# Expert parts that follow each other by halves of gate and up, and one-hot tables on VectorE

## The chip, the cores and the metric

The kernel runs on one core of a Trainium2 chip. The metric is the device time of one execution in microseconds. The kernel before takes 1694.38 us, the median of 3 runs (1686.91 to 1696.34).

The core has five engines that run beside each other, each through its own queue of instructions in order: TensorE (PE, matrix products, with its weight loads as PEld), VectorE (DVE), ScalarE (ACT), GpSimd (POOL) and SyncE (SP, which here only issues transfers). They meet through semaphores.

## The reference

One decoder block over 512 tokens of width 1024: a mixer (state-space scan and short convolution), then a mixture of experts with 64 experts, 8 for each token, expert width 256, and one shared expert. The change touches the experts alone. What they compute, shortened:

```python
scores = sigmoid(hf @ router_w)                       # 512 x 64
_, e_idx = lax.top_k(masked(scores + router_bias), 8)  # groups: 4 of 8 allowed
gate = take(scores, e_idx); gate = gate / gate.sum() * 2.5
def expert_block(xb, e):                               # rows of one expert
    return (silu(xb @ w_gate[e]) * (xb @ w_up[e])) @ w_down[e]
routed = segment_sum(yb * row_gate, row_tok)           # back to the tokens
shared = (silu(hf @ sh_gate) * (hf @ sh_up)) @ sh_down
x = layer_norm(ALPHA * x + g2 * (routed + shared)) * ln2_g + ln2_b
```

In float32, an expert's gate and up weights are 2 x 1 MB and its down weight 1 MB: 192 MB for the 64 experts, each read once.

## The kernel before

**Stages.** The mixer, the router and the shared expert fill the first 855 us or so. The routed experts run from about 876 to 1663 us, and the last layer norm ends the span.

**Parts and units.** The experts are ranked by their number of tokens, and each rank has a fixed number of rows (`CAPS`, L35). One tile of PE has 128 rows, so experts of few rows share a tile. A part is named by a letter: `q` is four experts of 32 rows in one tile, `p` two of 64, `a` one of 96 with one of 32, `f` one of 128; `y` is one expert of 192 rows, and `z` one of 160, each as a full tile of 128 (its block of one expert) and a second tile that it shares with another expert; `x` is the largest with three tiles. A unit is a few parts that are worked together: L41 names them, as `qy`, `ap` or `qff`. A static unit of experts 0 and 1 goes first. A block is one tile of rows, and a unit has one to four.

**What a unit does on PE**, in an order written by hand (`unit`, L1399, under the manual schedule of L1426): the products with gate and up (the first stage of `ffn`, L953 to L972), then, interleaved, the combination of the unit before (`csteps`, L1170, its products L1180 and L1181), this unit's transposes (`act_t`), and the gathering and transposing of the next unit's rows (`slots` L1101, `xs_steps` L1345), and then the products with the down weights. The gate and up products sum over K = 1024 in eight steps of 128, by quarters of two steps: a loop over four quarters `q` (L960), and in each all blocks of the unit, in the order of the unit in even quarters and backwards in odd ones. Blocks of several experts use plain products (`tiled`, L950, written to `ps_pj` or, for a fourth block, to `ps_y`). Blocks of one expert split each weight into a high and a low part (`split`, ACT L158 then DVE L160, three sets of buffers) and use three fast products for each step (L153, L154, L155). The other engines' instructions are ordered by a scheduler.

**Weights.** An expert's weights come in three pieces of 1 MB: half 0 and half 1 of gate and up (two transfers of 512 KB, L869) and down (L872). SP issues them in the order of the plan (`plan`, `take`; L1337 to L1339): all half-0 pieces of a unit, then all half-1 pieces, then all downs. There are buffers for nine pieces (seven `pr` and two more that every eighth piece takes), so a piece waits on SP until the one eight places before it has been read. Up to `AHEAD` = 10 are asked for early. The number of a routed expert is loaded on SP into a register (L1273) before its pieces can be issued.

**Rows in and out.** For each block DVE makes a one-hot table of the slots (`oh`, L1108), PE reduces it (L1116), DVE forms `idx` (L1121), and GpSimd issues the indirect transfer that gathers the rows (L1124). When a block's down product is done, `done` (L1143) makes on GpSimd a token number (`tok`, L1152) and the one-hot table `oht` of 128 x 512 (L1153) with which the next unit's combination adds the rows to the tokens. `oht` has three buffers, and one comes free when the combination that reads it has ended.

The line on which the order of a part's blocks rests, and the two on GpSimd:

```python
for o, (xh, xl), b in list(zip(os_, xs, blocks))[::-1 if q % 2 else 1]:
    ...
GP.tensor_scalar(tok, red[:, 0:1], NOTOK, None, op0=OP.add)
GP.tensor_scalar(res_[b][0], iota_t, tok, None, op0=OP.is_equal)
```

## Time and profile before

| | |
|---|---|
| median of 3 runs | 1694.38 us (1686.91 to 1696.34) |
| profiled execution | 1693.0 us |
| its span | 1691.2 us, mean granted clock of PE 0.95 |
| busy: PE, DVE, ACT, POOL | 1527.4, 962.3, 642.4, 315.9 us |

The profile is of one execution. Its span is 1.8 us shorter than that execution's own time, and the median of the three runs is 1.4 us longer than the profiled execution. Each row of a timeline below gives start and length in us, the engine and the line of the kernel, output and input by the program's names, and in square brackets the idle time just before the instruction with what ended it. PE's granted clock stands as a share of its full 2.4 GHz.

### The profile page before, as it was taken

How to read it: one execution, taken by the hardware profiler on the slowest of the kernel's cores; microseconds unless marked ns; L12 is line 12 of the kernel's file. 1: busy time of each engine (PE TensorE's matmuls, PEld its weight loads, DVE VectorE, ACT ScalarE, POOL GpSimd, SP SyncE). 2: the span in 40 equal slices, each digit the busy share in tenths (PEclk: the TensorE clock that was granted, in tenths of full speed). 3: DMA queues.
4: the chain of work that ended last, by engine and by line, in shares of the span. 5: the costliest groups of instructions: out<-in, count | busy, mean ns of one | idle time of the engine just before them, and what ended most of it. 6: DMA issues, size and time to landing. Idle time of an engine off the chain costs nothing.

```text
span 1691.2 us, 22909 instructions
## 1 busy us (share of the span) xinstructions
PE 1527.4 (90%) x8253; PEld 1024.9 (61%) x8253; DVE 962.3 (57%) x1728; ACT 642.4 (38%) x925; POOL 315.9 (19%) x314
## 2 busy tenths in 40 slices
PE   6999999999999999999887779997889988999894
PEld 4687787777878777877654344444434444544452
DVE  4558767777676666267853434345354453444445
ACT  3557656655535454344422222123231222212222
POOL 0011101101004566000350120221022211022111
PEclk9999999999999999999898879998799989999997
DMA  9663434425315576253537478776688769787671
GB/s 277 154 173 78 110 90 97 115 76 159 69 47 163 176 247 188 87 189 142 191 101 260 144 264 333 287 287 227 258 302 297 278 240 361 282 312 279 243 307 51
DMA packets 194504, 335.67 MB, mean 198 GB/s; under 512 B 13428, under 2 KB 136660, under 8 KB 186196
## 3 DMA queue, kind: packets, MB, share of 16 engines
q1 hardware_dynamic: 183300, 303.73, 52.7%
q0 software_dynamic: 11088, 30.45, 7.0%
q8 instruction: 66, 1.08, 0.3%
q14 instruction: 50, 0.41, 0.1%
HBM read 334.58 MB, written 4.28 MB: 200 GB/s over the span
## 4 chain that ended last, share of the span: by engine, by line
PE 68%; DMA 13%; DVE 7%; issue 6%; ACT 3%; POOL 2%; SPq 1%; DVEq 0%; POOLq 0%; ACTq 0%
PE ps_pj L153 12%; PE ps_pj L154 11%; PE ps_pj L155 11%; PE ps_pj L950 8%; DMA pr<-in_w_up_dram 6%; PE ps_y L950 5%; PE ps_tr L150 4%; PE ps_y L1180 4%; PE ps_y L1181 4%; DMA pg<-h_d,idx 4%; DMA pg<-in_w_ada_dram 2%; PE ps_y L153 1%; DVE wl L160 1%; PE ps_y L483 1%; POOL pg L366 1%
## 5 line engine op out<-in xcount | busy, mean ns | idle before, releaser
L153 PE MATMUL ps_pj<-hm,wh 128*128 128x512 f32 x680 | 274.9, 405 | 1.6 <-ACT wh L158 1.6
L155 PE MATMUL ps_pj<-hm,wl 128*128 128x512 f32 x680 | 266.7, 393 | 5.3 <-DVE wl L160 5.3
L154 PE MATMUL ps_pj<-hm,wh 128*128 128x512 f32 x680 | 266.6, 392 | 0.0
L950 PE MATMUL ps_pj<-pr,xt 128*32 128x512 f32 (+1 forms) x1472 | 226.4, 609 | 26.1 <-DMA pr<-in_w_up_dram 25.4
L160 DVE TENSOR_TENSOR wl<-pg,wh 128x1024 fp32r<-128x1024 f32 (+1 forms) x129 | 159.3, 1241 | 112.7 <-ACT wh L158 112.4
L160 DVE TENSOR_TENSOR wl<-pr,wh 128x1024 fp32r<-128x1024 f32 x72 | 85.9, 1221 | 163.2 <-ACT wh L158 163.2
L158 ACT ACTIVATE wh<-pg 128x1024 fp32r<-128x1024 f32 (+1 forms) x135 | 127.5, 952 | 132.2 <-PE ps_pj L154 98.9
L950 PEld LDWEIGHTS ps_pj<-pr,xt 128*32 128x32 f32 (+1 forms) x1472 | 61.8, 117 | 173.0 <-issue 167.4
L1153 POOL TENSOR_SCALAR oht<-iota_t,tok 128x512 fp32r<-128x512 f32 x41 | 76.9, 1879 | 472.6 <-PE ps_y L1181 470.5
L153 PEld LDWEIGHTS ps_pj<-hm,wh 128*128 128x128 f32 x680 | 128.0, 188 | 35.9 <-issue 6.6
L155 PEld LDWEIGHTS ps_pj<-hm,wl 128*128 128x128 f32 x680 | 127.9, 188 | 34.7 <-DVE wl L160 7.0
L154 PEld LDWEIGHTS ps_pj<-hm,wh 128*128 128x128 f32 x680 | 128.2, 188 | 28.8 <-issue 3.4
L158 ACT ACTIVATE wh<-pr 128x1024 fp32r<-128x1024 f32 x72 | 73.3, 1051 | 180.0 <-DMA pr<-in_w_down_dram 80.8
L150 PE MATMUL ps_tr<-ident,pg 128*128 128x128 f32 x392 | 72.2, 318 | 64.1 <-DMA pg<-h_d,idx 60.2
L1186 DVE TENSOR_TENSOR res<-res,ps_y 128x512 f32<-128x512 f32 x120 | 82.2, 686 | 56.2 <-PE ps_y L1181 55.0
L950 PE MATMUL ps_y<-pr,wkr 128*32 128x512 f32 (+1 forms) x736 | 111.8, 643 | 0.8 <-DVE wk L1157 0.8
L150 PEld LDWEIGHTS ps_tr<-ident,pg 128*128 128x128 f32 x392 | 59.7, 197 | 77.3 <-issue 44.2
L1157 DVE SCALAR_TENSOR_TENSOR wk<-ps_y,red,pg 128x512 f32<-128x512 f32 x82 | 60.8, 748 | 44.4 <-PE ps_y L155 25.9
L366 POOL TENSOR_TENSOR pg<-pg 128x1024 f32<-128x1024 f32 x28 | 75.4, 2708 | 53.7 <-ACT pg L364 53.7
L1124 POOL DMA_INDIRECT pg<-h_d,idx x41 | 46.4, 1132 | 177.2 <-issue 120.6
L153 PE MATMUL ps_pj<-pg,wh 128*128 128x512 f32 x192 | 75.9, 395 | 1.1 <-ACT zs L431 1.1
L155 PE MATMUL ps_pj<-pg,wl 128*128 128x512 f32 x192 | 76.2, 397 | 0.0
(394 smaller groups left out, 2682.0 us busy)
## 6 DMA issues: line engine op xcount, KB each, us to landing
pr<-in_w_gate_dram SPq DMA_DIRECT2D x128, 512.0 KB, 7.9
pr<-in_w_up_dram SPq DMA_DIRECT2D x128, 512.0 KB, 8.7
pr<-in_w_down_dram SPq DMA_DIRECT2D x64, 1024.0 KB, 11.0
pg<-in_w_in_dram SPq DMA_DIRECT2D x88, 512.0 KB, 6.2
pg<-in_w_ada_dram SPq DMA_DIRECT2D x48, 512.0 KB, 5.7
bc<-acs_d POOLq DMA_DIRECT2D x32, 256.0 KB, 4.2
pg<-in_w_ssd_out_dram SPq DMA_DIRECT2D x16, 512.0 KB, 4.5
pg<-in_w_sc_out_dram SPq DMA_DIRECT2D x8, 512.0 KB, 4.1
```

The source lines that it names most:

```text
L150: return PE.transpose(o, i, ident[:n, :n])
L153: PE.matmul(o, lh, rh, start=start, stop=False)
L154: PE.matmul(o, lh, rl, start=False, stop=False)
L155: PE.matmul(o, ll, rh, start=False, stop=stop)
L158: S.activation(hi, src, AF.Copy)
L160: V.tensor_tensor(lo, src, rw(hi), op=OP.subtract)
L366: GP.tensor_tensor(part[i], part[i], w, op=OP.add)
L950: PE.matmul(o[w * i:w * i + w, :], x[:, w * i:w * i + w], m, start=start, stop=stop, tile_position=(0, w * i))
L1153: GP.tensor_scalar(res_[b][0], iota_t, tok, None, op0=OP.is_equal)
L1180: PE.matmul(o, oh_, yh[:, ns_], start=(i == 0), stop=False)
L1181: PE.matmul(o, oh_, yl[:, ns_], start=False, stop=(i == len(ps_) - 1))
L1186: V.tensor_tensor(ra[t][:, ns_], ra[t][:, ns_], o, op=OP.add)
```

## The change

Each part of a unit is now a list of blocks (`subs`), and `halves_of` orders the gate and up products: every part does its half 0 of K (four steps) in turn, and then every part its half 1 in reverse order of parts and blocks. The splits of both quarters of a half are asked for before its products. A block's activation (`act_in`) follows its half 1 at once, so that the activations come in that order too. The plan asks for the pieces of a unit in the order in which the halves come, and for all downs behind them. `tok` and `oht` are made on VectorE (`V`) instead of GpSimd (`GP`). The shared expert and the static unit go through the same function, with one part. In the diff below three one-line hunks are left out, which pass the new argument.

```diff
--- before.py
+++ after.py
@@ -950,34 +950,42 @@
             PE.matmul(o[w * i:w * i + w, :], x[:, w * i:w * i + w], m, start=start, stop=stop,
                       tile_position=(0, w * i))
 
-    def ffn(blocks, xs, w, done, gp=False):
+    def halves_of(subs):
+
+        return [(s_, 0) for s_ in subs] + [(s_[::-1], 1) for s_ in subs[::-1]]
+
+    def ffn(blocks, subs, xs, w, done, gp=False):
+
 
 
 
         es = sorted({e for b in blocks for e in b})
         split_e = sorted({b[0] for b in blocks if len(b) == 1})
         os_ = [bank(*(("pj", 3) if i < 3 else ("y", 2))) for i in range(len(xs))]
-        for q in range(4):
-            uq = {e: w(e, q) for e in es}
-            hl_ = {e: split(uq[e], GP if gp else None) for e in split_e}
-            for o, (xh, xl), b in list(zip(os_, xs, blocks))[::-1 if q % 2 else 1]:
-                for k in (2 * q, 2 * q + 1):
+        sgs = {}
+        for s_, h in halves_of(subs):
+            uq = {(e, q): w(e, q) for e in sorted({e for i in s_ for e in blocks[i]}) for q in (2 * h, 2 * h + 1)}
+            hl_ = {eq: split(u, GP if gp else None) for eq, u in uq.items() if eq[0] in split_e}
+            for i in s_:
+                o, (xh, xl), b = os_[i], xs[i], blocks[i]
+                for k in range(4 * h, 4 * h + 4):
                     if len(b) == 1:
-                        wh, wl = hl_[b[0]]
+                        wh, wl = hl_[b[0], k // 2]
                         matmul3(o, xh[:, k, :], xl[:, k, :], wh[:, :, k % 2, :], wl[:, :, k % 2, :], k == 0, k == KD - 1)
                     else:
-                        tiled(o, xh[:, k, :], [uq[e][:, :, k % 2, :] for e in b], k == 0, k == KD - 1)
-            if q == 3:
-                sgs = [act_in(o) for o in os_]
+                        tiled(o, xh[:, k, :], [uq[e, k // 2][:, :, k % 2, :] for e in b], k == 0, k == KD - 1)
+                if h:
+                    sgs[i] = act_in(o)
             yield
-        acts = []
-        for sg, b in zip(sgs, blocks):
-            acts.append(act_t(sg, len(b) > 1))
+        acts = {}
+        for i, sg in sgs.items():
+            acts[i] = act_t(sg, len(blocks[i]) > 1)
             yield
         yield
         us = [{e: w(e, 4 + j) for e in es} for j in range(2)]
         wdn = {e: [split(us[j][e], GP if gp else None) for j in range(2)] for e in split_e}
-        for i, ((ah, al), b) in enumerate(zip(acts, blocks)):
+        for i, b in enumerate(blocks):
+            ah, al = acts[i]
             for n in range(2):
                 o = bank("y", 2)
                 ns_ = slice(n * 512, (n + 1) * 512)
@@ -1136,7 +1144,7 @@
 
     npart, tail = [0], [False]
 
-    def expert(blocks, sl_, xs, w):
+    def expert(blocks, subs, sl_, xs, w):
 
         res_ = []
@@ -1149,8 +1157,8 @@
                 res_.append((rt.tile([P, T], FR, name="oht", bufs=3), *ring[i]))
                 npart[0] += 1
                 tok = rt.tile([P, 1], F32, name="tok", bufs=2)
-                GP.tensor_scalar(tok, red[:, 0:1], NOTOK, None, op0=OP.add)
-                GP.tensor_scalar(res_[b][0], iota_t, tok, None, op0=OP.is_equal)
+                V.tensor_scalar(tok, red[:, 0:1], NOTOK, None, op0=OP.add)
+                V.tensor_scalar(res_[b][0], iota_t, tok, None, op0=OP.is_equal)
             _, yh, yl = res_[b]
             ns_ = slice(n * 512, (n + 1) * 512)
             yg = wk()
@@ -1162,7 +1170,7 @@
             if n == 1:
                 parts.append(res_[b])
 
-        return ffn(blocks, xs, rows_of(w), done)
+        return ffn(blocks, subs, xs, rows_of(w), done)
 
     parts = []
     rsum = rt.tile([P, NT, 2], F32, name="rsum")
@@ -1323,20 +1331,22 @@
                              [(tuple(range(m)), lambda r=r, n=n, m=m: slots(seg(r, n, m)))]))
     for ks in ORDER.split():
 
-        rs, bl = (), []
+        rs, bl, subs = (), [], []
         for k in ks:
             r_, b_ = kinds[k].pop(0)
+            subs.append(list(range(len(bl), len(bl) + len(b_))))
             bl += [(tuple(len(rs) + e for e in es), sl_) for es, sl_ in b_]
             rs += r_
-        units.append((rs, bl))
+        units.append((rs, bl, subs))
     assert not any(kinds.values())
     ublk, allb = {}, []
     for n, u in enumerate(units):
         ublk[n] = len(allb)
         allb += u[1]
-        for q in range(3):
-            for i, r in enumerate(u[0]):
-                plan((n, i, q), lambda r=r, q=q: expert_piece(rank(r), q))
+        if u[0]:
+            for i, q in [(i, h) for s_, h in halves_of(u[2]) for i in sorted({e for b in s_ for e in u[1][b][0]})] \
+                    + [(i, 2) for i in range(len(u[0]))]:
+                plan((n, i, q), lambda r=u[0][i], q=q: expert_piece(rank(r), q))
     xs = []
 
     def need_s(n):
@@ -1403,8 +1413,8 @@
         i0, i1 = ublk[n], ublk[n] + len(units[n][1])
         i2 = i1 + len(units[n + 1][1]) if n + 1 < len(units) else i1
         need_x(i1)
-        run = expert([b for b, _ in units[n][1]], sl[i0:i1], xs[i0:i1], lambda e, q: take((n, e, q), AHEAD))
-        for _ in range(4):
+        run = expert([b for b, _ in units[n][1]], units[n][2], sl[i0:i1], xs[i0:i1], lambda e, q: take((n, e, q), AHEAD))
+        for _ in range(2 * len(units[n][2])):
             next(run)
         com = csteps() if parts else iter(())
         for _ in range(2):
```

The first place is PE at the start of the first `ap` unit after the static one: the downs of `ya`, then all gate and up products of `ap` (64-row products are those of `p`, 32-row products those of `a`; `ps_y` holds downs, `ps_pj` gate and up, `xt` the gathered rows). Before:

```order
L950 MATMUL ps_y<-pr,wkr 64x512 x8
L950 MATMUL ps_y<-pr,wkr 32x512 x16
L950 MATMUL ps_pj<-pr,xt 32x512 x8
L950 MATMUL ps_pj<-pr,xt 64x512 x8
L950 MATMUL ps_pj<-pr,xt 32x512 x16
L950 MATMUL ps_pj<-pr,xt 64x512 x8
L950 MATMUL ps_pj<-pr,xt 32x512 x8
L1180 MATMUL ps_y<-rww,oht 128x512
```

And after:

```order
L950 MATMUL ps_y<-pr,wkr 64x512 x8
L950 MATMUL ps_y<-pr,wkr 32x512 x16
L950 MATMUL ps_pj<-pr,xt 32x512 x16
L950 MATMUL ps_pj<-pr,xt 64x512 x16
L950 MATMUL ps_pj<-pr,xt 32x512 x16
L1188 MATMUL ps_y<-rww,oht 128x512
L1189 MATMUL ps_y<-pg,oht 128x512
```

The first 32-row stretch has doubled, the two 64-row stretches have become one, and the pieces of half 1 of `a` are needed last instead of in the third and fifth stretch.

The second place is DVE behind the combination in the unit `qy` (`res` is the running sum of a token tile, `red` and `idx` belong to the slots of the next unit, `wl` to a split). Before:

```order
L1186 TENSOR_TENSOR res_75<-res_75,ps_y 128x512
L1119 TENSOR_REDUCE red<-ps_st 128x2
L1108 TENSOR_TENSOR oh<-iota_5824,pgt 128x512
L1121 TENSOR_SCALAR idx<-red 128x1
L160 TENSOR_TENSOR wl_79<-pr,wh_78 128x1024
L1186 TENSOR_TENSOR res_75<-res_75,ps_y 128x512
L1119 TENSOR_REDUCE red<-ps_st 128x2
L160 TENSOR_TENSOR wl_81<-pr,wh_80 128x1024
L1121 TENSOR_SCALAR idx<-red 128x1
```

And after:

```order
L1194 TENSOR_TENSOR res_75<-res_75,ps_y 128x512
L1127 TENSOR_REDUCE red<-ps_st 128x2
L1116 TENSOR_TENSOR oh<-iota_5824,pgt 128x512
L1129 TENSOR_SCALAR idx<-red 128x1
L1161 TENSOR_SCALAR oht<-iota_t,tok 128x512 x2
L1194 TENSOR_TENSOR res_75<-res_75,ps_y 128x512
L160 TENSOR_TENSOR wl_79<-pr,wh_78 128x1024
L1127 TENSOR_REDUCE red<-ps_st 128x2
L1160 TENSOR_SCALAR tok<-red 128x1
L160 TENSOR_TENSOR wl_81<-pr,wh_80 128x1024
L1129 TENSOR_SCALAR idx<-red 128x1
L1161 TENSOR_SCALAR oht<-iota_t,tok 128x512
```

Two tables stand behind the first `idx` and ahead of the last sum of the combination, and a third behind the second `idx`. On POOL, where tables and gathers took turns, nothing but the gathers is left.

The third place is SP before the routed experts (`L869` and `L872` are pieces of the static unit, `eidx` the list of expert numbers). Before:

```order
L869 DMA pr<-in_w_up_dram 128x1024
L872 DMA pr<-in_w_down_dram 128x2048 x2
L1273 TENSOR_LOAD eidx
L1273 ISA x2
L869 REGISTER_ALU
L869 ISA
L869 DMA pr<-in_w_gate_dram 128x1024
```

And after:

```order
L869 DMA pr<-in_w_up_dram 128x1024
L1281 TENSOR_LOAD eidx
L1281 ISA x2
L1281 TENSOR_LOAD eidx
L1281 ISA x2
L1281 TENSOR_LOAD eidx
L1281 ISA x2
L1281 TENSOR_LOAD eidx
L1281 ISA x2
L1281 TENSOR_LOAD eidx
L1281 ISA x2
L1281 TENSOR_LOAD eidx
```

Six loads of expert numbers, which wait for `eidx`, now stand ahead of the other three gate and up pieces and the two downs of the static unit.

## Rows read from the trace of the kernel before

**Rows 1.** The page: the span and the busy times of the engines.

```profile
span 1691.2 us, 22909 instructions
...
PE 1527.4 (90%) x8253; PEld 1024.9 (61%) x8253; DVE 962.3 (57%) x1728; ACT 642.4 (38%) x925; POOL 315.9 (19%) x314
```

**Rows 2.** Busy time of each engine in three stretches: the routed experts, the gate and up products of `qy`, and those of `qff`. The columns are start and end, length, busy us and count of PE, PEld, DVE, ACT and POOL, PE's granted clock, the share of the transfer engines that is busy, and GB/s.

```profile
900.00:1660.00 760.00, 671.69 (x4048) 359.83 (x4048) 337.20 (x562) 191.81 (x307) 118.79 (x110) 0.92 0.73 270
953.60:989.60 36.00, 27.65 (x123) 9.48 (x121) 4.63 (x6) 3.27 (x4) 0.00 (x0) 0.81 0.64 234
1169.50:1212.90 43.40, 31.72 (x116) 15.20 (x108) 11.43 (x11) 8.64 (x9) 0.00 (x0) 0.69 0.64 228
```

**Rows 3.** What PE waited for between 900 and 1660 us: us in total, times, longest.

```profile
PE ps_tr L150 <- DMA pg<-h_d,idx: 52.0, 10, 8.1
PE ps_pj L950 <- DMA pr<-in_w_up_dram: 25.4, 14, 6.5
PE ps_pj L153 <- ACT wh L158: 3.8, 4, 2.3
PE ps_pj L154 <- DVE wl L160: 2.6, 5, 0.8
```

**Rows 4.** The timeline of PE in the gate and up products of `qff`, up to the first product of the combination (L1180). L950 is `q`, L153 to L155 are the two `f`.

```profile
1169.46 1.90 PE L950 MATMUL ps_pj<-pr,xt 128*32 128x512 f32 x16
1173.63 0.50 PE L153 MATMUL ps_pj<-wh,xt 128*128 128x512 f32 x1 [2.27 <-ACT wh L158]
...
1193.05 1.89 PE L950 MATMUL ps_pj<-pr,xt 128*32 128x512 f32 x2 [4.58 <-DMA pr<-in_w_up_dram]
1196.12 3.59 PE L950 MATMUL ps_pj<-pr,xt 128*32 128x512 f32 x10 [1.19 <-DMA pr<-in_w_up_dram]
...
1211.08 1.92 PE L950 MATMUL ps_pj<-pr,xt 128*32 128x512 f32 x16
1212.93 0.50 PE L1180 MATMUL ps_y<-pr,oht 128*128 128x512 f32 x1
```

**Rows 5.** The timeline of SP's queue in the same stretch: the last half-0 piece, the first transfer of the half-1 pieces of `q`, and the downs behind them.

```profile
1172.06 0.34 SPq L869 DMA_DIRECT2D pr<-in_w_up_dram  x1
1187.63 0.33 SPq L869 DMA_DIRECT2D pr<-in_w_gate_dram  x1
...
1193.48 22.36 SPq L872 DMA_DIRECT2D pr<-in_w_down_dram  x6
```

**Rows 6.** The timeline of PE in the gate and up products of `qy`: the second tile of `y` (64 columns) in one quarter, and `q`'s waits.

```profile
957.03 3.65 PE L950 MATMUL ps_pj<-pr,xt 128*64 128x512 f32 x16
...
971.44 1.89 PE L950 MATMUL ps_pj<-pr,xt 128*32 128x512 f32 x2 [6.46 <-DMA pr<-in_w_up_dram]
974.71 3.59 PE L950 MATMUL ps_pj<-pr,xt 128*32 128x512 f32 x10 [1.39 <-DMA pr<-in_w_up_dram]
```

**Rows 7.** The timeline of PE: the first and the last of the ten waits for a weight of gate and up in the other units.

```profile
1041.04 1.49 PE L950 MATMUL ps_pj<-pr,xt 128*32 128x512 f32 x12 [0.79 <-DMA pr<-in_w_up_dram]
...
1609.53 2.78 PE L950 MATMUL ps_pj<-pr,xt 128*32 128x512 f32 x24 [1.54 <-DMA pr<-in_w_up_dram]
```

**Rows 8.** What POOL waited for between 860 and 1660 us, the largest entry: us in total, times, longest.

```profile
POOL oht L1153 <- PE ps_y L1181: 470.5, 11, 62.2
```

**Rows 9.** The timeline of POOL: the issue of a gather (DMA_INDIRECT) in the unit before `qy`, and a table with the gather behind it in `qy`.

```profile
936.67 0.99 POOL L1124 DMA_INDIRECT pg<-h_d,idx  x1 [31.67 <-PE ps_st L1116]
...
1003.03 2.63 POOL L1153 TENSOR_SCALAR oht<-iota_t,tok 128x512 fp32r<-128x512 f32 x1 [57.22 <-PE ps_y L1181]
1005.82 1.14 POOL L1124 DMA_INDIRECT pg<-h_d,idx  x1 [0.16 <-issue]
```

**Rows 10.** The timeline of DVE: the indices of those two gathers.

```profile
935.78 0.15 DVE L1121 TENSOR_SCALAR idx<-red 128x1 int32<-128x1 f32 x1
...
1002.92 0.15 DVE L1121 TENSOR_SCALAR idx<-red 128x1 int32<-128x1 f32 x1
```

**Rows 11.** The timeline of PE: the transposes that wait for the second of them.

```profile
1011.32 1.94 PE L150 MATMUL ps_tr<-ident,pg 128*128 128x128 f32 x8 [6.83 <-DMA pg<-h_d,idx]
```

**Rows 12.** Groups of DVE instructions of one line and shape in the whole span: count, busy us, mean ns of one, idle us before them.

```profile
L468 DVE TENSOR_SCALAR esc<-bc,acs 128x128 f32<-128x128 f32 x128 | 29.9, 292 | 6.1 <-DMA bc<-acs_d 5.4 <-PE ps_y L483 0.7
L258 DVE TENSOR_SCALAR pg<-pg,mv,rstd 128x1024 f32<-128x1024 f32 x4 | 3.2, 804 | 0.0
L1121 DVE TENSOR_SCALAR idx<-red 128x1 int32<-128x1 f32 x41 | 6.1, 148 | 0.1
```

**Rows 13.** The timeline of SP's queue at the first routed pieces: between the second and the third transfer stands one load of an expert's number.

```profile
856.28 0.36 SPq L869 DMA_DIRECT2D pr<-in_w_gate_dram  x1
856.90 0.34 SPq L869 DMA_DIRECT2D pr<-in_w_up_dram  x1
858.17 0.34 SPq L869 DMA_DIRECT2D pr<-in_w_gate_dram  x1
```

**Rows 14.** The timeline of PE: the first gate and up product of the static unit.

```profile
876.13 1.93 PE L950 MATMUL ps_pj<-pr,xt 128*64 128x512 f32 x6
```

**Rows 15.** The page's groups: the two steps of a weight's split.

```profile
L160 DVE TENSOR_TENSOR wl<-pr,wh 128x1024 fp32r<-128x1024 f32 x72 | 85.9, 1221 | 163.2 <-ACT wh L158 163.2
...
L158 ACT ACTIVATE wh<-pr 128x1024 fp32r<-128x1024 f32 x72 | 73.3, 1051 | 180.0 <-DMA pr<-in_w_down_dram 80.8
```

**Rows 16.** A short stretch with a brief wait for a weight, in the columns of rows 2.

```profile
1085.00:1095.00 10.00, 9.14 (x39) 3.76 (x40) 1.25 (x3) 0.66 (x2) 0.00 (x0) 0.83 0.94 383
```

More of the change, by code (lines that the diff above doesn't have):

```diff
@@ L1226, in done @@
             GP.tensor_tensor(ra[ts[b]][:, ns_], ra[ts[b]][:, ns_], tm, op=OP.add)
-        drain(ffn([[0]] * len(ts), [mt[t] for t in ts], lambda e, q: shw[q], done, len(ts) > 1))
+        drain(ffn([[0]] * len(ts), [list(range(len(ts)))], [mt[t] for t in ts], lambda e, q: shw[q], done, len(ts) > 1))
     def static_slots(u):
@@ L1302, in block_kernel @@
     of = {c: [r for r in range(E - NST) if caps[r] == c] for _, c in CAPS}
-    units = [((), [(tuple(range(len(u))), lambda u=u: static_slots(u))]) for u in STAT]
+    units = [((), [(tuple(range(len(u))), lambda u=u: static_slots(u))], [[0]]) for u in STAT]
     kinds = {c: [] for c in "xyzfapq"}
@@ L1503, in block_kernel @@
         blk = slots((pv[:, :, None], P, [po]))
-        drain(expert([[0]], [blk], [xsplit(blk[0])], lambda e, q: expert_piece(bass.ds(er, 1), q)))
+        drain(expert([[0]], [[0]], [blk], [xsplit(blk[0])], lambda e, q: expert_piece(bass.ds(er, 1), q)))
         combine(True)
```

## The prediction

> **What bounds the kernel now.** I read the page first. PE is busy 1527 of 1691 us [rows 1], so some 164 us can be won at most, and a change of the experts only finds its part of it between 900 and 1660 us. There PE is busy 672 of 760 us; DVE has 337 us of work and is free for 423, POOL has 119, and the transfers take 0.73 of their engines' time [rows 2]. No engine but PE is full over the whole stretch. Then I read what PE waits for there [rows 3]: 52 us for gathered rows (ten times), 25 us for weights of gate and up (14 times), and 6.4 us for splits. The last stretches to read are the two units with four experts in `q`, because the granted clock is 0.81 in the gate and up products of `qy` and 0.69 in those of `qff`, against 0.92 over all routed experts [rows 2]. A level of 0.5 (1.2 GHz) thus holds for much of both. So a wait costs twice there: once itself, and again in slower products behind it.
>
> **Gate and up of `qff`.** They take from 1169.46 to 1212.93, that is 43.5 us [rows 4]. PE alone at full clock needs 18.7: four quarters of `q` at 1.9 (the row of 16 products), and for each `f` 24 split products of 0.232 us (the distance from start to start of the fast ones), two times 5.6. The loss begins with the weights. Six half-0 pieces come first, and the half-1 pieces of `q` need the buffers from which half 0 of `q` is read. With the quarters taken in turn, that half is read out only when the second quarter of `q` ends, and SP issues the first of them at 1187.63 [rows 5]. PE waits from 1188.5 to 1193.05, once more to 1196.12, and then goes on at half speed [rows 4]. After the change `q` does its two quarters of half 0 in one go, from 1169.5 to 1173.3, so those four buffers come free 14.3 us earlier, while both `f` are worked. The transfers do not follow by as much. The last half-0 piece is issued at 1172.06 [rows 5] and three to four pieces of 1.05 MB are still on their way. At 383 to 400 GB/s, the rate of a full stretch [rows 16], a piece takes 2.7 us; four behind four are done some 20 us after 1171, at about 1192. One half of `q`, 3.8 us, may follow the last: 1196 to 1198 in place of 1212.9. I take 15 us less. The best is PE alone with the first split in its way, 23 less. The worst has splits as the limit: eight pairs of DVE subtractions at 1.22 us [rows 15] are 19.5 us, from 1173 to 1192, and `q` at half clock behind them, 7.6, would end at 1200; with a late piece, 10 less.
>
> **Gate and up of `qy`.** They take 36.0 us [rows 2]; PE alone needs 7.6 for `q`, 5.6 for the full tile of `y` and 7.3 for its second tile, 3.65 for each of two quarters' worth of pairs [rows 6], 20.5 in sum. Half 0 of `q` would be read out at 957.4 and its pieces' successors issued from there, before the 12.9 us of `y`, which end at 970.3. The four pieces (10.5 us behind some that are on the way) would be in at about 972, and the end at 976 and not at 989.6: 13 us less. At most 15, which is PE alone; at least 6, if only the wait of 6.46 goes [rows 6].
>
> **The other waits for weights.** Ten in seven units, such as 0.79 in the first and 1.54 in the last [rows 7]. When the four of `qff` and `qy` are taken from the 25.4 us of rows 3 (4.58, 1.19, 6.46 and 1.39), 11.8 are left. In an `ap` unit the second part's weights of half 1 are wanted before those of the first, and the gap between half 0 of `a` and its half 1 grows by a whole part, 3.65 us; a weight that was late by 0.8 to 1.5 us would then be in time. A stretch with such a wait ran at 0.83 [rows 16], so a little clock returns. I take 9, with bounds of 3 and 15.
>
> **Tables off POOL.** POOL runs its queue in order. A table waits for its buffer, which the last product of the combination frees: 470 us in eleven waits [rows 8]. A gather behind it is late though its index is there. In the unit before `qy` an index begins at 935.78 and its gather is issued at 936.67, 0.9 later; in `qy` an index begins at 1002.92, two-and-a-half microseconds of table follow, and the gather goes at 1005.82, 2.9 later [rows 9, 10]. PE waits for its rows until 1011.32, for 6.83 us [rows 11]. So 2.0 of that go. I did the same for each of the ten waits in rows 3: six gathers stand behind a table, with 1.0 to 2.7 us lost, 10 in all; four lose nothing. The rest of the 52 us is the gather's own latency and stays. I take 10; none if something else holds the gather, and 13 with the clock.
>
> **Tables on DVE.** 41 tables of 128x512 from one operand. No row has this operation on DVE; its like took 292 ns at a quarter of the size and 804 ns at twice it [rows 12], so I take 0.5, and the token number as 0.15. All on the path that would be 27 us. They are covered: DVE is free for 423 of 760 us [rows 2], and behind the combination, where they stand, PE waits for the gather, not for DVE. The first index stands ahead of the first two tables, so it isn't late; the second index stands behind them, by 1.0 to 1.6 us, less than a table took on POOL. I take 0, bounds 0 and 5.
>
> **SP before the routed experts.** Six loads of an expert's number move ahead of five pieces of the static unit. One costs the distance from 856.90 to 858.17 [rows 13], less that of a plain pair (0.62), some 0.65 us; with a bound of 0.93 the five extra ones are 3.3 to 4.7 us. The pieces that now go out by 840 would go out from about 860 and, at 2.7 us each, be in by 871 to 874; the first product that wants one is at 876.13 [rows 14], and downs come later. So 0, up to 5 if the clear space of 2 to 5 us is used up.
>
> **Order of splits and activations.** A half asks for two pairs of splits with three sets of buffers, in the shared expert, too; and the activations come backwards, which the combination hides. I take 1 more, between 1 less and 4 more.
>
> The sum goes against the profiled execution's 1693.0: less 15, 13, 9 and 10, plus 1, is 46 less, 1647. The median stands 1.4 higher, hence 1648. With every best bound it is 67 less, 1627; with every worst, 5 less, 1689.
>
> **A rule from the skill.** A gather issued beside a DVE split of 1.22 us took 1.14 us against 0.99 [rows 9], and that split has two operands in the SBUF. The Trainium skill, page "SBUF — State Buffer", section "SBUF: two separate sides", says that a DVE operation in a two-port mode keeps GpSimd from writing the descriptors of its transfers; page "VectorE: DVE Perf Modes", section "The perf-mode tier table", gives such a mode to `tensor_scalar` on float32. By that rule the two tables just behind an index would hold up the gather that the index has released. No row shows this pair; what it would take is below.
>
> **Rivals.**
> Transfers stay the limit in the six-expert units. For it: the half-1 pieces come in a queue that is already full at 383 GB/s [rows 16]. Against: over these two stretches the share is 0.64 [rows 2]. Then half of 28 and 3 of 9 remain: 1668.
> More returns: no wait for weights is left, and the clock stays up. All best bounds: 1628.
> Two tables beside the gather's issue take back the 2.0 us that it won: no gain at the gathers, and so 1658. The rule above is the reason; only 0.15 us is seen so far.
> Nothing comes of it: the waits only gather elsewhere, since a combination that starts earlier meets the same gathers and downs still on their way (they go out in a run of 22 us, [rows 5]); about 1690.
> Slower: splits. A full tile now wants two quarters' splits at once, with three sets; if the scheduler starts them only when the part begins, PE stands for a whole chain of ACT and DVE, about 2.5 us (1.05 and 1.22 for each of two, overlapped [rows 15]; the wait at 1173.63 was 2.27 [rows 4]). Twelve experts with full tiles, two halves each: 60 us. It decides when the chains aren't ahead in more than three quarters of the cases: 1693 less 46 plus 60, with the 1.4, is 1708. Against it: all splits together cost PE 6.4 us so far [rows 3], and the wait of 2.27 stood behind a late weight.
>
> **How the numbers follow.** Forecast 46% (its own range 1638 to 1661), transfers 20%, tables beside the gather 8%, more returns 10%, nothing 9%, slower 7%. About 0.5% (8.5 us, 1686 to 1703) is what a measurement of this kernel can tell from no change. Faster by more has the first four, 84%; same 9%; slower 7%. The range leaves out the slower case and half of the extreme ones: 1628 to 1686.
>
> **What would show it.** In the changed profile: the SP timeline of `qff` should issue `q`'s half-1 pieces about 4 us behind the first product, not 18; the stretch from the first product to the combination should be near 28 us, with a clock above 0.8, and that of `qy` near 23. PE's waits for gate and up should be under 8 us in place of 25, those for gathers near 42. POOL should wait for no table. Splits should cost PE no more than 10 us. If gathers are issued over 1.5 us behind their index, the rule on ports is at work; if the downs or the gathers wait longer than before, the gain went there, and I am wrong.

## The result and the profile after

The changed kernel takes 1629.8 us, the median of 4 runs (1629.3 to 1630.8); the kernel before took 1692.2 in the same comparison. The ratio is 0.963, with a 95% interval of 0.960 to 0.966. The profiled execution took 1629.3 us, and its span is 63.7 us shorter. 1648 was forecast, so the direction and the range held (1628 to 1686), but the gain was 62 us and not 46.

The page of the changed kernel, as [rows 1]:

```profile
span 1627.5 us, 22863 instructions
...
PE 1496.8 (92%) x8253; PEld 1018.3 (63%) x8253; DVE 974.6 (60%) x1810; ACT 645.4 (40%) x925; POOL 230.3 (14%) x232
```

PE executes the same 8253 products and is busy 30.6 us less, so about half of the gain is products that run at a faster clock. The windows of the changed kernel over the routed experts, `qy` and `qff`, in the columns of [rows 2], show where: the clock is 0.94 and 1.00 where it was 0.81 and 0.69.

```profile
900.00:1600.00 700.00, 639.24 (x4034) 353.32 (x4033) 354.15 (x637) 195.45 (x308) 39.17 (x35) 0.96 0.78 293
945.80:973.30 27.50, 24.52 (x122) 9.29 (x120) 5.52 (x8) 4.04 (x6) 0.00 (x0) 0.94 0.94 352
1141.20:1167.60 26.40, 21.11 (x116) 11.03 (x108) 12.34 (x13) 9.67 (x11) 0.00 (x0) 1.00 1.01 380
```

PE's waits in the changed kernel between 900 and 1600 us, as [rows 3] (the routed experts end 64 us earlier now, hence the shorter stretch): weights 9.7 us instead of 25.4, gathered rows 43.7 instead of 52.0, splits 5.7 instead of 6.4.

```profile
PE ps_tr L150 <- DMA pg<-h_d,idx: 43.7, 11, 5.4
PE ps_pj L950 <- DMA pr<-in_w_up_dram: 9.7, 8, 1.6
PE ps_pj L154 <- DVE wl L160: 4.8, 6, 1.0
...
PE ps_pj L153 <- ACT wh L158: 0.9, 2, 0.5
```

Then I cut both timelines of PE at the first product of each stage (gate and up, combination, downs) and took the lengths from one to the next:

| stage | before | after | change, us |
|---|---|---|---|
| start of the static unit | 876.1 | 877.3 | +1.1 |
| static unit to `x` | 30.5 | 19.8 | -10.7 |
| `x` | 47.0 | 48.8 | +1.8 |
| gate and up of `qff` | 43.5 | 26.5 | -17.0 |
| gate and up of `qy` | 36.0 | 27.5 | -8.5 |
| gate and up of the other units | 237.9 | 222.9 | -15.0 |
| combinations behind `x`, with transposes and gathers | 252.5 | 240.1 | -12.4 |
| downs behind `x` | 137.7 | 134.4 | -3.3 |
| sum | | | -64.0 |

Each column is one execution. The start of the static unit alone lies anywhere from 875.5 to 884.4 us in the profiles of this study, so a difference of 1 or 2 us in one row says little.

The timeline of PE in the gate and up products of `qff` in the changed kernel, as [rows 4]:

```profile
1141.16 3.62 PE L950 MATMUL ps_pj<-pr,xt 128*32 128x512 f32 x32
1145.28 0.49 PE L153 MATMUL ps_pj<-wh,xt 128*128 128x512 f32 x1 [0.50 <-ACT wh L158]
...
1161.47 1.04 PE L950 MATMUL ps_pj<-pr,xt 128*32 128x512 f32 x2 [1.60 <-DMA pr<-in_w_up_dram]
1164.10 3.59 PE L950 MATMUL ps_pj<-pr,xt 128*32 128x512 f32 x26 [1.58 <-DMA pr<-in_w_up_dram]
1167.62 0.51 PE L1188 MATMUL ps_y<-pr,oht 128*128 128x512 f32 x1
```

And SP's queue there, as [rows 5]: the first and the last transfer of `q`'s four half-1 pieces, and the downs.

```profile
1144.78 0.34 SPq L869 DMA_DIRECT2D pr<-in_w_gate_dram  x1
...
1153.33 0.34 SPq L869 DMA_DIRECT2D pr<-in_w_up_dram  x1
1155.06 12.91 SPq L872 DMA_DIRECT2D pr<-in_w_down_dram  x6
```

The first half-1 piece of `q` goes out 3.6 us behind the first product, where it was 18.2. PE still waits for the last of them, two times 1.6 us, and here the clock stays up behind them: the last 26 products take 3.59 us where 10 took that long in [rows 4]. In `qy` it does not stay up behind waits of this length, as is shown further down.

### The profile page after: what moved, and what is told of

Its sections match the earlier page's. It is cut to its first block, busy times and chain, and to the rows that moved or that the text cites. A ratio compares the mean times of both kernels' runs of the same rounds, so it can differ in the third digit from the quotient of the medians.

```text
span 1627.5 us, 22863 instructions
## 1 busy us (share of the span) xinstructions
PE 1496.8 (92%) x8253; PEld 1018.3 (63%) x8253; DVE 974.6 (60%) x1810; ACT 645.4 (40%) x925; POOL 230.3 (14%) x232
## 4 chain that ended last, share of the span: by engine, by line
PE 68%; DMA 12%; DVE 8%; issue 6%; ACT 3%; POOL 1%; SPq 1%; DVEq 0%; ACTq 0%; POOLq 0%
PE ps_pj L153 12%; PE ps_pj L154 12%; PE ps_pj L155 12%; PE ps_pj L950 6%; DMA pr<-in_w_up_dram 5%; PE ps_y L950 5%; PE ps_y L1188 4%; PE ps_y L1189 4%; PE ps_tr L150 4%; DMA pg<-h_d,idx 4%; DMA pg<-in_w_ada_dram 2%; DVE wl L160 2%; PE ps_y L153 1%; PE ps_y L155 1%; PE ps_y L154 1%
## 5 line engine op out<-in xcount | busy, mean ns | idle before, releaser
L153 PE MATMUL ps_pj<-hm,wh 128*128 128x512 f32 x680 | 276.3, 407 | 2.0 <-ACT wh L158 2.0
L155 PE MATMUL ps_pj<-hm,wl 128*128 128x512 f32 x680 | 267.4, 394 | 6.2 <-DVE wl L160 6.2
L950 PE MATMUL ps_pj<-pr,xt 128*32 128x512 f32 (+1 forms) x1472 | 212.2, 604 | 9.7 <-DMA pr<-in_w_up_dram 9.7
L950 PEld LDWEIGHTS ps_pj<-pr,xt 128*32 128x32 f32 (+1 forms) x1472 | 62.0, 117 | 150.1 <-issue 139.7
L153 PEld LDWEIGHTS ps_pj<-hm,wh 128*128 128x128 f32 x680 | 128.9, 190 | 36.7 <-issue 6.0
L155 PEld LDWEIGHTS ps_pj<-hm,wl 128*128 128x128 f32 x680 | 128.5, 189 | 36.7 <-DVE wl L160 8.8
L950 PE MATMUL ps_y<-pr,wkr 128*32 128x512 f32 (+1 forms) x736 | 106.1, 618 | 0.8 <-DVE wk L1165 0.8
L927 ACT ACTIVATE sg<-ps_pj 128x256 f32<-128x256 f32 x44 | 16.8, 384 | 159.7 <-PE ps_pj L950 99.2
L153 PE MATMUL ps_pj<-pg,wh 128*128 128x512 f32 x192 | 76.0, 396 | 1.3 <-ACT zs L431 1.2
L155 PE MATMUL ps_pj<-pg,wl 128*128 128x512 f32 x192 | 76.3, 397 | 0.0
```

What stands on the lines that cost most here:

```text
L153: PE.matmul(o, lh, rh, start=start, stop=False)
L155: PE.matmul(o, ll, rh, start=False, stop=stop)
L950: PE.matmul(o[w * i:w * i + w, :], x[:, w * i:w * i + w], m, start=start, stop=stop, tile_position=(0, w * i))
```

## The experiments

**The order alone, the tables alone.** In the first, the new order has the tables back on GpSimd; in the second, the kernel before has them on VectorE.

```diff
-                V.tensor_scalar(tok, red[:, 0:1], NOTOK, None, op0=OP.add)
-                V.tensor_scalar(res_[b][0], iota_t, tok, None, op0=OP.is_equal)
+                GP.tensor_scalar(tok, red[:, 0:1], NOTOK, None, op0=OP.add)
+                GP.tensor_scalar(res_[b][0], iota_t, tok, None, op0=OP.is_equal)
```

> The new order of parts, with the one-hot tables left on GpSimd. Theory: the two halves of the change add up, and the order is worth what the stages of gate and up lost in the changed kernel: 17 us in qff, 8.5 in qy and some 15 in the other units, about 41 of the 62, so 1651 us with 1692 before; the static stage before the unit x should again last about 30 us from its first gate and up product to that of x, and PE should wait for gathers as before, about 52 us. Rival: the static stage and the gathers got faster because the weights come in another order and leave the transfer engines free at other times, and the tables matter little; then this kernel takes about 1632 us and the static stage about 20 us.

> The old order of parts, with the one-hot tables on VectorE. Theory: the gathers no longer stand behind tables; the static stage loses about 10 us and the combinations about 12, so some 22 less than before: 1670 us; qff keeps its 43.5 us of gate and up. Rival (the weights' order frees the transfer engines): about 1690 us, static stage still 30 us.

The order alone: 1649.0 us, ratio 0.975 (0.972 to 0.978), 42 us by the ratio and 43 by the medians. The tables alone: 1677.6 us, 0.993 (0.991 to 0.995), 12 us by the ratio and 15 by the medians, where 22 were expected. Together that is 54 to 58 of the 62, the rest within the intervals. The waits between 900 and 1600 us part as foretold, the order alone first:

```profile
PE ps_tr L150 <- DMA pg<-h_d,idx: 53.4, 10, 8.1
PE ps_pj L950 <- DMA pr<-in_w_up_dram: 11.0, 11, 2.0
```

and then the tables alone:

```profile
PE ps_tr L150 <- DMA pg<-h_d,idx: 45.6, 10, 6.8
PE ps_pj L950 <- DMA pr<-in_w_up_dram: 22.5, 11, 5.0
```

The order took the weights' waits, the tables the gathers'. Cut in the same way as in the table above, the order alone has 27.5 us in `qff`, 27.2 in `qy`, 223.9 in the other gate and up products and 252.9 in the combinations; the tables alone have 43.0, 33.2, 231.6 and 244.8. So the order has nearly all of its gain in gate and up. The tables have theirs in the combinations, but 6 us in the other gate and up products too.

One thing fits neither theory: the static stage was 23.7 us in both. The order alone still makes the tables on GpSimd there, but in its profile the second one took 1.65 us, where it took 2.71 before:

```profile
885.20 1.65 POOL L1161 TENSOR_SCALAR oht<-iota_t,tok 128x512 fp32r<-128x512 f32 x1
```

So its first gather left only 0.29 us behind the first weight and landed after 8.9 us; what this says comes below. Why the table was shorter is not shown.

**The other two corners.** Order of work and order of pieces are two edits. In the third kernel PE works in the new order and the pieces come in the old one; in the fourth PE works by quarters and the pieces come in the new order. The tables are on VectorE in both.

```diff
-            for i, q in [(i, h) for s_, h in halves_of(u[2]) for i in sorted({e for b in s_ for e in u[1][b][0]})] \
-                    + [(i, 2) for i in range(len(u[0]))]:
-                plan((n, i, q), lambda r=u[0][i], q=q: expert_piece(rank(r), q))
+            for q in range(3):
+                for i, r in enumerate(u[0]):
+                    plan((n, i, q), lambda r=r, q=q: expert_piece(rank(r), q))
```

> The changed kernel with the pieces planned as before (all half 0, all half 1, all downs) while PE works in the new order. Theory A (the order of the pieces is needed too): in qff the pieces of half 1 of f stand behind four of q in SP's queue, and PE wants them first, so qff loses 8 to 14 of its 17 us and qy some 5, with a few us in the others: 1645 to 1655. Theory B (only the early reading of half 0, which frees the buffers, counts): within 5 us of the changed kernel, 1628 to 1635.

```diff
-        for s_, h in halves_of(subs):
-            uq = {(e, q): w(e, q) for e in sorted({e for i in s_ for e in blocks[i]}) for q in (2 * h, 2 * h + 1)}
+        for q in range(4):
+            uq = {e: w(e, q) for e in es}
...
```

> The fourth corner: PE works by quarters as before, the pieces come in the new order, and the tables are on VectorE. Theory (order of work and order of pieces only help together): PE wants half 1 of q in the third quarter, but it is last in SP's queue and needs the buffers of half 0, so the waits for weights are longer than in the kernel with the tables alone (1678): 1690 to 1720. Rival (the order of the pieces is the whole gain): about 1640.

1698.0 us (ratio 1.004, 1.001 to 1.006) and 1714.6 us (1.012, 1.008 to 1.015). Either edit alone loses where both win 48: beside the 1677.6 of the tables alone, the loss is 20 and 37 us (18 and 32 by the ratios). Both theories about the third kernel missed the time. Theory A was right where it named a size: `qff` takes 36.0 us, 9.5 more than in the changed kernel, and `qy` 34.3, 6.8 more. But the other gate and up products, for which it had a few us, take 270.0, and that is 47 more. All of PE's waits for weights there are 44.8 us in 21 waits, where the changed kernel has 9.7 in 8. In `qff` PE stands before the second half of an `f`:

```profile
1188.99 0.79 PE L153 MATMUL ps_pj<-wh,xt 128*128 128x512 f32 x1 [11.48 <-ACT wh L158]
```

ACT waits there for the piece that is behind four of `q` in the queue; the row names ACT, but the weight is what came late. In the fourth kernel, too, most of the loss lies outside of the place that was named. `q` does wait in the third quarter of `qff`, but `qff` takes 43.6 us and took 43.0 with the tables alone. The other gate and up products take 269.5 in place of 231.6, and 7 and 8 us of that are in the two `faa` units, where half 1 of `f` is wanted in the third quarter and now comes last. PE's row names ACT, and ACT's row the weight:

```profile
1413.63 0.79 PE L153 MATMUL ps_pj<-wh,xt 128*128 128x512 f32 x1 [7.15 <-ACT wh L158]
```

```profile
1412.52 2.00 ACT L158 ACTIVATE wh<-pr 128x1024 fp32r<-128x1024 f32 x2 [14.41 <-DMA pr<-in_w_up_dram]
```

**The static stage.** The first four tables alone (static unit and `x`) are put on VectorE in the kernel before.

```diff
-                GP.tensor_scalar(tok, red[:, 0:1], NOTOK, None, op0=OP.add)
-                GP.tensor_scalar(res_[b][0], iota_t, tok, None, op0=OP.is_equal)
+                (V if npart[0] <= 4 else GP).tensor_scalar(tok, red[:, 0:1], NOTOK, None, op0=OP.add)
+                (V if npart[0] <= 4 else GP).tensor_scalar(res_[b][0], iota_t, tok, None, op0=OP.is_equal)
```

> The kernel before with the first four one-hot tables alone (those of the static unit and of x) on VectorE. Theory: the static stage (first gate and up product of the static unit to that of x) loses 30.5 us to about 20 to 24, because its first gather no longer stands behind two tables on GpSimd and goes out ahead of the weights that the static unit's products release, and all later units stay as before: 1682 to 1686 us with 1692 before. Rival: the short static stage of the changed kernel comes from the pieces that are issued later there, not from the tables; then 1692 and 30 us.

1685.3 us, ratio 0.994 (0.992 to 0.996), and the static stage is 23.7 us; what else brings it to 19.8 when the order is changed too was not tried. By the ratios that is 10 us (6 to 14) for four tables of 41, and 12 (8 to 16) for all of them, so the first four have most of the gain. The profiled execution (1695.6 us) is the longest of this kernel's eight: its static stage is 6.8 us shorter than before, but starts 5.0 later, so it shows the stage and not where the 10 us of the median lie. The first gather of `x` tells why the stage is shorter. Before, it left behind a table, at 882.83, when the static unit's products had already released weights, the first at 881.48; the row of transfers gives 12.8 us from its issue to its landing:

```profile
882.83 1.67 POOL L1124 DMA_INDIRECT pg<-h_d,idx  x1 [0.17 <-issue]
```

```profile
881.48 0.34 SPq L869 DMA_DIRECT2D pr<-in_w_gate_dram  x1
```

```profile
pg<-h_d,idx POOLq DMA_INDIRECT x1, 12.8
```

After, it left at 881.56, the first weight at 882.44, and it landed in 6.2:

```profile
881.56 1.52 POOL L1132 DMA_INDIRECT pg<-h_d,idx  x1 [4.29 <-DVE tok L1160]
```

```profile
882.44 0.33 SPq L869 DMA_DIRECT2D pr<-in_w_gate_dram  x1
```

```profile
pg<-h_d,idx POOLq DMA_INDIRECT x1, 6.2
```

To try this by itself, the changed kernel got two operations ahead of that one gather, which write the buffer that the gather overwrites and so can't fall behind it.

```diff
+        if nblk[0] == 1:
+            for i in range(2):
+                GP.tensor_scalar(xg[:, i * T:(i + 1) * T], iota_t, red[:, 0:1], None, op0=OP.add)
```

> The changed kernel with two extra operations of 128x512 on GpSimd right ahead of the first gather of the static stage (they fill the buffer that the gather then overwrites), some 3.4 us, as the two tables were there before. In the kernel before, that gather was issued 1.35 us behind the first weight that the static unit's products released, and landed after 12.8 us; in the changed kernel it was issued 0.88 us ahead of it and landed after 6.2. Theory (behind the weights it waits for them, so 3.4 us on GpSimd cost twice that): landing 11 to 13 us, static stage 26 to 30 us in place of 19.8, 6 to 10 us more in all, 1636 to 1640. Rival (the landing depends on something else of the old order): landing 6 to 8 us, static stage 22 to 23 us, 3 us more.

1637.0 us, 7 more than the changed kernel; the ratio is 0.968 (0.963 to 0.972), and its interval overlaps that of the changed kernel. The stages are clearer than the sum: the static stage is 28.8 us, 9.0 more, and `x` behind it 45.1, 3.7 less. In the order of time, from its timelines: the first weight, the gather, the transposes.

```profile
884.43 0.33 SPq L869 DMA_DIRECT2D pr<-in_w_gate_dram  x1
```

```profile
882.57 3.16 POOL L1133 TENSOR_SCALAR pg<-iota_t,red 128x512 f32<-128x512 f32 x2 [3.31 <-DVE red L1127]
886.00 2.12 POOL L1135 DMA_INDIRECT pg<-h_d,idx  x1 [0.27 <-POOL pg L1133]
```

```profile
898.70 1.94 PE L150 MATMUL ps_tr<-ident,pg 128*128 128x128 f32 x8 [8.59 <-DMA pg<-h_d,idx]
```

It left 1.57 us behind the weight and took 12.6 to land. So 3.2 us on GpSimd cost 9 in the stage, and 5 in the two stages together.

**Tables twice.** Each table is made twice on VectorE in the changed kernel.

```diff
                 V.tensor_scalar(res_[b][0], iota_t, tok, None, op0=OP.is_equal)
+                V.tensor_scalar(res_[b][0], iota_t, tok, None, op0=OP.is_equal)
```

> The changed kernel with each one-hot table made twice on VectorE, 41 more instructions of some 0.5 us. Theory (they lie beside waits of VectorE): 0 to 5 us more, 1630 to 1635. Rival (they stand on the path, behind the index or ahead of the last sums): 41 by 0.5 is 20 us more, 1650. If a table beside the issue of a gather blocks it, the issue comes over 1.3 us behind the index instead of 0.9.

1635.0 us against 1629.8 in another comparison, but the ratio to before is the same, 0.964 (0.961 to 0.967). So 41 more operations cost nothing that these runs can tell, and not the 20 us of the rival. One table takes 0.485 us on average in the changed kernel, near the 0.5 assumed. In this kernel one issue of a gather lies beside tables for 0.86 of its 0.99 us:

```profile
1130.02 0.15 DVE L1129 TENSOR_SCALAR idx<-red 128x1 int32<-128x1 f32 x1
1130.08 0.87 DVE L1161 TENSOR_SCALAR oht<-iota_t,tok 128x512 fp32r<-128x512 f32 x2
1130.87 0.89 DVE L1162 TENSOR_SCALAR oht<-iota_t,tok 128x512 fp32r<-128x512 f32 x2
```

```profile
1130.90 0.99 POOL L1132 DMA_INDIRECT pg<-h_d,idx  x1 [1.66 <-DVE oht L1161]
```

The gather goes 0.88 us behind its index and its issue takes 0.99, as without tables [rows 9, 10].

**The gathers that are left.** Of PE's waits, 44 us for gathers were the largest. The first trial swapped the combination steps between this unit's transposes for transposes of the next unit's rows.

```diff
+        nxt = xs_steps(i2)
         for _ in range(i1 - i0):
             next(run)
-            next(com, None)
-        zipper(xs_steps(i2), com, islice(over_, 1))
+            next(nxt, None)
+        zipper(nxt, com, islice(over_, 1))
```

> The changed kernel with the transposes of the next unit's rows taken in the places of combination steps right after this unit's own transposes, and the combination steps put behind them, so that more steps of the combination lie behind the issue of a gather. Theory: PE's 46 us of waits for gathers are bare latency of about 4 to 5 us each that has no work on PE behind it; with combination steps there 20 to 40 us go: 1590 to 1610. Rival: the latency only moves, because the third gather of a unit waits for its buffer and the splits of the gathered rows are late: 1620 to 1632.

It failed: 1675.5 us, ratio 0.990 (0.987 to 0.992), 46 more than the changed kernel. The third block's rows were wanted after three of the eight combination steps, while five lay unused behind them, and PE stood in `qff`:

```profile
1207.60 1.09 PE L150 MATMUL ps_tr<-ident,pg 128*128 128x128 f32 x4 [7.44 <-DMA pg<-h_d,idx]
```

All waits for gathers rose from 43.7 to 56.5 us; of the other 33 us, new waits of transposes for ScalarE (6.6) are a part, and the rest was not taken apart. The third gather can't leave early: its slots stand in PE's order behind the transposes of the first block (`xs_steps`). So the first block has to come at the very start, and the third at the very end:

```diff
+        nxt = xs_steps(i2)
         for _ in range(2):
-            next(com, None)
+            next(nxt, None)
         for _ in range(i1 - i0):
             next(run)
             next(com, None)
-        zipper(xs_steps(i2), com, islice(over_, 1))
+        for _ in range(2):
+            next(nxt, None)
+            next(com, None)
+        zipper(com, islice(over_, 1))
+        drain(nxt)
```

> The changed kernel with the first gathered block of the next unit transposed at the start of the stage between gate and up and the downs, its second in the middle, all combination steps then, and its third block last. So five or more combination steps stand between the issue of the third block's gather and its transposes. Theory: most of the 46 us of waits for gathers go: 1595 to 1608. Rival: like the former trial, in which the transposes came at other places and the waits for gathers rose to 56 us, since the gathers are late for another reason (their slots wait for VectorE or for their buffer): 1630 to 1675.

1616.9 us, ratio 0.954 (0.951 to 0.957): 13 us better than the changed kernel, half of what was expected. The waits of this kernel between 900 and 1600 us:

```profile
PE ps_tr L150 <- DMA pg<-h_d,idx: 14.2, 8, 3.4
...
PE ps_tr L150 <- DVE xt L160: 7.7, 8, 1.0
```

30 us of waits went, 8 came new: transposes that follow each other directly wait for VectorE to empty their buffers. That leaves 9 us of the difference without an account. With one combination step between the two first steps:

```diff
-        for _ in range(2):
-            next(nxt, None)
+        next(nxt, None)
+        next(com, None)
+        next(nxt, None)
```

> The kernel of the last trial (first gathered block early, third block last) with one combination step between the two first transpose steps. Theory: at the start of the stage PE waits there about 1 us a unit for VectorE to empty the transpose buffers (7.7 us in all); the step between covers this, and one step less behind the third gather costs little: 3 to 8 us less than the last trial's 1616.9, so 1609 to 1614. Rival: the waits for gathers (14 us) grow by as much: 1615 to 1622.

1609.1 us, ratio 0.950 (0.947 to 0.953), as expected, though the gathers' waits grew to 24.3 us, as the rival had it. The kernel without the step, run again beside a later trial, gave 0.955 (0.952 to 0.959):

> The kernel with the first gathered block early and the third last, once more beside the other, to see how far its time and that of the version with one step between (1609.1) are apart when the kernel before is the same chip's. Theory: 5 to 8 us above 1609 by the ratio to before, 0.953 to 0.956. Rival: the same within the interval, 0.950.

The intervals touch, so that the step is worth some 6 us is likely, not settled. Both are faster than the changed kernel.

## Why the prediction was right, and where it was short

**The ceiling.** The prediction's "some 164 us can be won at most" took PE's busy time as fixed. It is not, since it holds slow products: 30.6 us of it went with the same products.

**Weights of `qff`: right.** 15 was said, 17 came. The buffers came free about when it was worked out (3.6 us behind the first product), and the end lies 26.5 us behind the start, 26.5 to 28.5 by the working.

**Weights of `qy`: too large.** 13 was said, 8.5 came. The pieces were reckoned to be in 18.4 us behind the first product; PE went on with the last at 968.08, 22.3 behind its start at 945.83:

```profile
945.83 3.64 PE L950 MATMUL ps_pj<-pr,xt 128*32 128x512 f32 x32
...
965.64 1.02 PE L950 MATMUL ps_pj<-pr,xt 128*32 128x512 f32 x2 [1.56 <-DMA pr<-in_w_up_dram]
968.08 5.32 PE L950 MATMUL ps_pj<-pr,xt 128*32 128x512 f32 x26 [1.42 <-DMA pr<-in_w_up_dram]
```

The rate was 352 GB/s over the stretch, not the 383 to 400 of the sum. It was not low at the end (410 from 961 us on), but at the start, 203 in the first 4.2 us. The term was also too large by the clock: these last 26 products take 5.32 us, and in `qff` 26 take 3.59. The granted clock fell to 0.50 behind the waits of 1.56 and 1.42, in the columns of [rows 2]:

```profile
962.00:968.00 6.00, 3.10 (x8) 0.42 (x6) 0.42 (x1) 0.38 (x1) 0.00 (x0) 1.00 1.03 419
969.00:971.00 2.00, 2.00 (x16) 0.52 (x12) 0.00 (x0) 0.00 (x0) 0.00 (x0) 0.50 1.02 426
```

Here, and with the two short waits of `qff`, the first rival has a share: with a transfer share of 0.94 and 1.01 these units are now bound by transfers. All waits for gate and up are 9.7 us, where under 8 was to be seen.

**Other weights: 9 was said, 15 came**, the upper bound. The gate and up products of the first `ap` alone became 4.1 us shorter, where the trace of before has this wait:

```profile
1085.86 4.73 PE L950 MATMUL ps_pj<-pr,xt 128*64 128x512 f32 x13 [1.64 <-DMA pr<-in_w_up_dram]
```

That stretch ran at 0.83 [rows 16], so the clock's return is the likely remainder; it was not tried by itself. Not all of the 15 is the order's: the tables alone took 6 us off these stages.

**Gathers in the later units: right in kind.** 10 was said; PE's waits fell by 8.3, and the stage by 12.4.

**The static stage: missed.** The prediction let the change find its part "between 900 and 1660 us" alone, so a stage that ends at 907 and gave 10.7 us was outside the sum, although the gather there stood behind two tables like the others. The term for gathers counted only the time that the issue lost. The trials show the other price: a gather that leaves 1.4 or 1.6 us behind released weights lands 6 us later. `x` behind this stage lost 1.8, so the two together gave 8.9. The trace shows what `x` lost: its products now meet a gather that is still on its way, and run at a granted clock of 0.55 from 899.6 to 902.9.

```profile
899.65 0.95 PE L150 MATMUL ps_tr<-ident,pg 128*128 128x128 f32 x4 [1.90 <-DMA pg<-h_d,idx]
```

**Terms taken as nothing.** Tables on VectorE: so, as far as doubling them can tell. The loads of expert numbers on SP: the static unit's pieces went out from 861.7, PE waited for none, and the start of the unit moved by 1.1 us; other kernels of this study, with either order on SP, start it between 875.5 and 884.4, so no more can be said. The downs gave 3.3, and no term was there for it.

**Tables beside the gather's issue.** The gather is issued 0.88 or 0.89 us behind its index and at its usual length, so this rival fell. The rule of the Trainium skill that stood beside it ("SBUF — State Buffer", section "SBUF: two separate sides") does not show in this pair: the issue at 1130.90 in the kernel with doubled tables, and the one at 1319.64 in the changed kernel, lie beside tables for 0.86 and 0.85 us and take 0.99 both. Longer issues stand beside splits, 2.03 us at 1376.28 in the changed kernel.

**Rivals.** The slower one fell: PE's waits for splits went from 6.4 to 5.7 us, three sets were enough. More returns (1628) was the nearest, but for a reason that was not in it: more than half of the missing 18 us is the static stage, 10.7; 6 are other weights, 3.3 downs, 2.4 combinations and 2 `qff`, and 1 was set down for splits. Off that go 4.5 at `qy`, 1.8 at `x` and 1.1 at the start.

## What to carry to other kernels

When weights stream through few buffers, the order in which they are used and the order in which they are asked for are one decision: here both together won 48 us beside the tables alone, and either alone lost 20 or more. On an in-order queue that issues transfers, look for operations that wait for something else, and price them not by their own length but by what the transfer then queues behind. Before putting work into a gap, look what the issue of the late transfer waits for, and do that first.

## What was not expected of the hardware

In the static stage of ten profiles the first gather of 128 rows was issued 0.9 us ahead of a run of weight transfers from another queue, and landed after 6.1 to 7.4 us. In three it came behind the first of them: 0.29 us behind, it landed after 8.9; 1.57 and 1.35 behind, after 12.6 and 12.8. The next gather of the stage, 0.95 to 1.3 behind, landed after 8.3 to 10.2 in six of them, so the delay alone does not set the time. The clock was the other surprise: waits of 4.6 and 6.5 us [rows 4, 6] stood ahead of stretches at 0.5 in the kernel before, which its windows show in the columns of [rows 2]:

```profile
1193.00:1200.00 7.00, 5.48 (x12) 0.76 (x12) 0.00 (x0) 0.75 (x1) 0.00 (x0) 0.50 1.01 343
...
971.00:976.00 5.00, 3.18 (x10) 0.59 (x11) 0.00 (x0) 0.00 (x0) 0.00 (x0) 0.50 1.03 400
```

After the change, two waits of 1.6 us in `qff` stood ahead of none (granted clock 1.00 throughout), and two of 1.56 and 1.42 in `qy` of one at 0.50. What makes the difference is not shown.
